# Copies of x and the first eight splits ahead of the main loop's, a last bank in two halves, and stationary parts moved by 32 bytes

## The chip, the cores and the metric

The kernel runs on one core of a Trainium2 chip. The metric is the device time of one execution in microseconds (us), the median of several runs.

## What is computed

One layer of a decoder trunk on x of 256 tokens by 2048, in float32:

```
h = rms_norm(x, g_mix);  q, k, v of 16 heads = h @ w_in
x = x + concat(diff_attention, moba_attention, dilated_attention) @ w_out
x = x + memory_cross_attention(rms_norm(x), rms_norm(mem), w_cq, w_ckv, w_co)
x = x + (silu(causal_dwconv3(h @ w_gate)) * (h @ w_up_half)) @ w_down,  h = rms_norm(x, g_ffn)
out = rms_norm(x, g_final)
```

The weights w_in, w_out, w_ckv, w_cq, w_co, w_up and w_down come to some 220 MB and are read once.

## The kernel before, in words

**Products in parts.** A float32 operand is split into a high part (a copy rounded to float32r, made on ScalarE) and a low part (the remainder, made on VectorE). A product of two operands is the sum of high by high, high by low and low by high, all accumulated in one PSUM bank. Activations lie in hT with the high part of a block of 128 rows in the first 256 columns and the low part in the next 256.

**Pieces, halves and steps.** All weights are streamed in pieces of 1 MB (2048 columns of 128 partitions), each into one of four buffers raw (NRAW = 4), by SyncE's queue. A piece has two halves of 1024 columns. split_hi (line 142) casts a half on ScalarE, split_lo (line 149) makes its low part on VectorE; there are five buffers of each (NSPLIT = 5), so that half i waits until the matmuls of an earlier half have been done. The main loop (lines 1023 to 1040) has one step for each half: it allots and issues loads (line 127), splits the half that is LEAD = 4 ahead, runs what is due before the step, runs the matmuls of the step and then what is due after it. The functions before(i, f) and after(i, f) put work at those places. The order in which instructions are written is the order on each engine's queue; nothing reorders it.

**The start.** x comes in as 16 blocks of 128 by 256; a block is multiplied by its gain and split into hT on ScalarE (line 194) and VectorE (line 197); put_x does it for two blocks. The loads of x and of pieces 0 to 2 are written alternately on SyncE's queue, the load of piece 3 follows. A fourth buffer of raw is taken by a tile named hold: POOL writes one column of it (line 951), and VectorE copies that column before step 8 (line 952), which ends the tile's life. So piece 3 goes into piece 0's buffer, and so on. Blocks 0 to 3 and halves 0 and 1 are split ahead of the loop. Then lines 981 and 982 put two blocks of x and one half after each of the steps 0 to 5:

```
    for i in range(6):
        after(i, lambda i=i: (put_x(2 * i + 4), split(i + 2)))
```

The loop itself splits half 8 at step 4, half 9 at step 5 and so on, ahead of the step's matmuls; what is due after a step is written behind them.

The first group of 512 columns takes steps 0 to 7. In steps 0 to 2 the eight high matmuls of 512 columns (line 295) come first and then the eight low ones of 256 (line 302); from step 3 on they alternate in pairs. A group has four PSUM banks of a pool of five (NACC = 5). At the end of step 7 each bank is emptied by a copy on ScalarE (line 354) and an add on VectorE (line 355). Step 8 begins the next group of columns with four banks, the first of which is the fifth of the pool. Squares of x are summed beside steps 5 to 9 (line 223 on ScalarE, line 227 on VectorE).

**The down projection and the tail.** For it the activations are the stationary operand (ah, al, 128 by 128) and the weights the moving one, 512 columns at a time (lines 851 to 853). All eight banks hold outputs: two tiles of 128 tokens by four quarters of 512 columns. The last TAIL = 2 rows of blocks are kept back, and for each bank in turn their matmuls are run at the end, so that banks become ready one after the other. Each is added to x on VectorE (line 890) and squared and summed on ScalarE (line 265); after the last of a tile the sums give a factor (lines 899 to 901 on VectorE, a power on POOL at line 903), and finish multiplies each quarter by it and stores it. gains multiplies some quarters by g_final ahead of that (line 898).

**Places in memory.** A tile's place is rounded up to 32 bytes. The high and low weight parts hi and lo begin at a multiple of 64 bytes; hT, and in the down projection ah and al, begin 32 bytes past one. The tile gfin lies ahead of ah and al.

Of the kernel before, what the change touches and what calls it, by code (L numbers as in the profile page):

```python
# [11 lines left out]
F32 = mybir.dt.float32  # L12
# [50 lines left out]
def trunk(ctx, tc, x, mem, w_in, w_out, diff_lambda, rel_bias_table, w_cq, w_ckv, w_co, w_up, conv, w_down,  # L63
# [30 lines left out]
    def small(n, name, bufs=4):  # L94
        return tmp.tile([P, n], F32, tag=f"sm_{name}", name=name, bufs=bufs)
# [62 lines left out]
    def before(i, f):  # L158
        pre.setdefault(i, []).append(f)

    def after(i, f):
        post.setdefault(i, []).append(f)
# [100 lines left out]
    def square_sum(src, acc, n=512):  # L263
        junk = tmp.tile([P, 512], mybir.dt.bfloat16, tag="junk", name="junk", bufs=1)
        ACT.activation(junk[:, :n], src, AF.Square, accum_out=acc)
# [557 lines left out]
    def xtok(t, c):  # L823

        return xT[:, 4 * c + 2 * t:4 * c + 2 * t + 2, :].rearrange("p k n -> p (k n)")
# [17 lines left out]
        hi, lo = parts[k]  # L843
        DVE.tensor_tensor(lo, ffn["a"][:, k, :], hi.bitcast(F32), op=ALU.subtract)

    def down_mm(p, k, h, t, n):
        hi, lo = p.parts[h]
        ah, al = (a[:, t * P:(t + 1) * P] for a in parts[k])
        o = outs[t, 2 * h + n]
        wh, wl = hi[:, n * 512:(n + 1) * 512], lo[:, n * 512:(n + 1) * 512]  # L850
        PE.matmul(o, ah, wh, start=(k == 0), stop=False)  # L851
        PE.matmul(o, ah, wl, start=False, stop=False)  # L852
        PE.matmul(o, al, wh, start=False, stop=(k == KF - 1))  # L853

    ss3 = small(8, "ss3", 1)
    fin = {}

    def finish(n, t, og, r):
        col = slice(n * 512, (n + 1) * 512)
        if t and n % 2:  # L860
            DVE.scalar_tensor_tensor(og[:, col], xtok(t, n), r, gfin["t"][:, col], op0=ALU.mult, op1=ALU.mult)
        elif t or n < 2:
            ACT.activation(og[:, col], og[:, col], AF.Copy, scale=r)
        else:
            (DVE, POOL)[n - 2].tensor_scalar_mul(og[:, col], og[:, col], r)
        SP.dma_start(out[t * P:(t + 1) * P, col], og[:, col])

    def down(k):
        def f(p, h):
            if k == 0 and h == 0:  # L870
                for t in range(NT):
                    for n in range(4):
                        outs[t, n] = any_tile()
            fin[k] = p
            if k < KF - TAIL:
                for t in range(NT):
                    for n in range(2):
                        down_mm(p, k, h, t, n)
            elif k == KF - 1 and h == 1:
                done = None  # L880
                for t in range(NT):
                    og = wpool.tile([P, 2 * HALF], F32, tag="raw", name="raw", bufs=NRAW)
                    ms = small(2, "msf")
                    ss = ss3[:, 4 * t:4 * t + 4]
                    for n in range(4):
                        for kk in range(KF - TAIL, KF):
                            down_mm(fin[kk], kk, n // 2, t, n % 2)
                        col = slice(n * 512, (n + 1) * 512)
                        xc = xtok(t, n)
                        DVE.tensor_tensor(xc, outs[t, n], xc, op=ALU.add)  # L890
                        square_sum(xc, ss[:, n:n + 1])
                        if done:
                            for m in ((3, 0, 1), (2,), (), ())[n]:
                                finish(m, *done)
                        gains = ((), (0,), (), (2,)) if t else ((0,), (1,), (2,), (3,))
                        for m in gains[n]:
                            col = slice(m * 512, (m + 1) * 512)
                            DVE.tensor_tensor(og[:, col], xtok(t, m), gfin["t"][:, col], op=ALU.mult)
                    DVE.reduce_sum(ms[:, 0:1], ss[:, :3], axis=AX.X)
                    DVE.tensor_scalar(ms[:, 0:1], ms[:, 0:1], 1.0 / D, EPS, op0=ALU.mult, op1=ALU.add)  # L900
                    DVE.scalar_tensor_tensor(ms[:, 1:2], ss[:, 3:4], 1.0 / D, ms[:, 0:1], op0=ALU.mult, op1=ALU.add)
                    r = small(1, "rfin")
                    POOL.tensor_tensor(r, ms[:, 1:2], mhalf, op=ALU.pow)
                    done = t, og, r
                for n in range(4):
                    finish(n, *done)
        return f

# [4 lines left out]
    gfin = {}  # L913

    def load_final():
        gfin["t"] = ffn["p"].tile([P, D], F32, name="gfin")
        SP.dma_start(gfin["t"], bass.AP(tensor=g_final.tensor, offset=g_final.offset, ap=[[0, P], [1, D]]))

    after(startF + 10, load_final)
# [26 lines left out]
    load_x(12, 4)  # L946

    hold = wpool.tile([P, 2 * HALF], F32, tag="raw", name="raw", bufs=NRAW)  # L950
    POOL.memset(hold[:, :1], 0.0)
    before(8, lambda: DVE.tensor_copy(small(1, "held", 1), hold[:, :1]))


    warm = acc_tile()
    for _ in range(24):
        PE.transpose(warm[:, :P], ident, ident)
# [20 lines left out]
    split(1)  # L978
    load(pieces[3])
    nload = 4  # L980
    for i in range(6):
        after(i, lambda i=i: (put_x(2 * i + 4), split(i + 2)))
    for c in range(4):
        square_part(c + 5, "x", c, lambda c=c: xpart(c))
    norm_factors(10, "x")
# [87 lines left out]
```

## Time and profile before

| | us |
|---|---|
| median of 3 runs (1252.23 to 1252.81) | 1252.4 |
| the profiled execution | 1252.27 |
| its span, first to last instruction | 1250.5 |
| TensorE busy in the span | 1235.8 |
| VectorE busy | 830.8 |
| ScalarE busy | 630.0 |

The profile tells for one execution when each instruction began and how long it took. In its views PE is TensorE (matmuls), PEld its weight loads, DVE VectorE, ACT ScalarE, POOL GpSimd and SP SyncE. L149 is line 149 of the kernel, lo<-raw,hi says that the tile lo is written from raw and hi, and a bracket tells how long the engine was idle before and what ended that. Matmuls are pipelined: a matmul's duration is longer than the distance to the next one's start, and it is the distance that counts in a stream. Times in the views are from the start of the span.

### The profile page before, as it was taken

What the parts mean: (1) busy time and instruction counts of PE and PEld (TensorE: products, weight loads), DVE (VectorE), ACT (ScalarE), POOL (GpSimd) and SP (SyncE); (2) the same over time, 40 slices, a digit from 0 to 9 for tenths busy, and PEclk for the clock granted to TensorE, in tenths of its full rate; (3) what the DMA queues carried; (4) which work ended last, traced back from release to release, by engine and by line L of the source; (5) the groups of instructions that cost most, each with busy time, mean ns of one, the idle gap of its engine ahead of it and who ended that gap; (6) DMA issues with size and microseconds to landing.
All of it is one profiled execution on the core that took longest, in us unless ns stands there. A gap on an engine that the chain in (4) does not pass through costs nothing.

```text
span 1250.5 us, 17611 instructions
## 1 busy us (share of the span) xinstructions
PE 1235.8 (99%) x6928; PEld 1072.4 (86%) x6928; DVE 830.8 (66%) x1351; ACT 630.0 (50%) x979; POOL 12.3 (1%) x23
## 2 busy tenths in 40 slices
PE   8999999999999999999999999999999999999997
PEld 7888888988888899888888888888888888888885
DVE  5755676576568877876767768667776854445445
ACT  6544555556455656545445444444444544444444
POOL 0000000000000000000000000000000000000000
PEclk9999999999999999999999999999999999999998
DMA  7855554555566555565556565565556555555541
GB/s 275 273 172 191 189 170 159 182 184 156 177 227 217 170 169 164 204 206 169 170 201 196 175 202 190 183 201 184 187 180 202 192 193 180 200 176 194 187 150 68
DMA packets 104835, 233.26 MB, mean 187 GB/s; under 512 B 4208, under 2 KB 14768, under 8 KB 98992
## 3 DMA queue, kind: packets, MB, share of 16 engines
q1 hardware_dynamic: 104576, 231.85, 55.3%
q8 instruction: 54, 0.88, 0.3%
q10 hardware_dynamic: 144, 0.26, 0.1%
q14 instruction: 29, 0.24, 0.1%
q0 software_dynamic: 32, 0.02, 0.0%
HBM read 230.00 MB, written 2.12 MB: 186 GB/s over the span
## 4 chain that ended last, share of the span: by engine, by line
issue 58%; PE 37%; DMA 2%; DVE 2%; ACT 0%; POOL 0%; DVEq 0%; POOLq 0%; SPq 0%; ACTq 0%
PE acc L295 16%; PE acc L302 8%; PE acc L341 3%; PE acc L343 3%; PE acc L342 3%; DMA raw<-in_w_in 1%; PE at L401 1%; DMA xin<-in_x 1%; DVE lo L149 1%; PE at L420 0%; PE at L444 0%; DVE hT L197 0%; PE acc L298 0%; PE acc L297 0%; PE at L472 0%
## 5 line engine op out<-in xcount | busy, mean ns | idle before, releaser
L149 DVE TENSOR_TENSOR lo<-raw,hi 128x1024 fp32r<-128x1024 f32 x423 | 517.1, 1223 | 360.0 <-ACT hi L142 359.5
L142 ACT CAST hi<-raw 128x1024 fp32r<-128x1024 f32 x423 | 442.8, 1048 | 473.1 <-PE acc L295 272.4
L295 PE MATMUL acc<-hT,hi 128*128 128x512 f32 x1776 | 625.4, 395 | 3.5 <-ACT hi L142 3.3
L302 PE MATMUL acc<-hT,lo 128*128 128x256 f32 x1840 | 512.0, 280 | 0.6 <-DVE lo L149 0.6
L295 PEld LDWEIGHTS acc<-hT,hi 128*128 128x128 f32 x1776 | 334.4, 188 | 78.1 <-ACT hi L142 3.7
L302 PEld LDWEIGHTS acc<-hT,lo 128*128 128x128 f32 x1840 | 345.3, 188 | 1.4 <-DVE lo L149 1.2
L295 PE MATMUL at<-hT,hi 128*128 128x512 f32 x528 | 187.5, 392 | 0.0
L302 PE MATMUL at<-hT,lo 128*128 128x256 f32 x528 | 147.6, 280 | 0.0
L295 PEld LDWEIGHTS at<-hT,hi 128*128 128x128 f32 x528 | 99.1, 188 | 21.8
L302 PEld LDWEIGHTS at<-hT,lo 128*128 128x128 f32 x528 | 99.2, 188 | 0.0
L851 PE MATMUL acc<-hi,ah 128*128 128x512 f32 x220 | 87.8, 399 | 0.0
L853 PE MATMUL acc<-hi,al 128*128 128x512 f32 x220 | 86.7, 394 | 0.0
L852 PE MATMUL acc<-lo,ah 128*128 128x512 f32 x220 | 86.2, 392 | 0.0
L341 PE MATMUL acc<-hi,hT 128*128 128x256 f32 (+1 forms) x224 | 75.0, 335 | 0.0
L343 PE MATMUL acc<-hi,hT 128*128 128x256 f32 (+1 forms) x224 | 73.9, 330 | 0.0
L342 PE MATMUL acc<-lo,hT 128*128 128x256 f32 (+1 forms) x224 | 73.8, 330 | 0.0
L851 PE MATMUL at<-hi,ah 128*128 128x512 f32 x132 | 52.7, 399 | 0.0
L853 PE MATMUL at<-hi,al 128*128 128x512 f32 x132 | 52.0, 394 | 0.0
L788 ACT ACTIVATE y<-y 128x256 f32<-128x256 f32 x44 | 18.4, 419 | 66.3 <-DVE y L784 66.3
L852 PE MATMUL at<-lo,ah 128*128 128x512 f32 x132 | 51.7, 392 | 0.0
L853 PEld LDWEIGHTS acc<-hi,al 128*128 128x128 f32 x220 | 41.3, 188 | 10.8
L852 PEld LDWEIGHTS acc<-lo,ah 128*128 128x128 f32 x220 | 41.3, 188 | 9.8
(159 smaller groups left out, 1003.2 us busy)
## 6 DMA issues: line engine op xcount, KB each, us to landing
raw<-in_w_up SPq DMA_DIRECT2D x88, 1024.0 KB, 5.0
raw<-in_w_in SPq DMA_DIRECT2D x45, 1024.0 KB, 5.2
raw<-in_w_down SPq DMA_DIRECT2D x44, 1024.0 KB, 4.9
raw<-in_w_out SPq DMA_DIRECT2D x12, 1024.0 KB, 5.3
raw<-in_w_ckv SPq DMA_DIRECT2D x8, 1024.0 KB, 5.6
raw<-in_w_out SPq DMA_DIRECT2D x8, 512.0 KB, 4.9
raw<-in_w_cq SPq DMA_DIRECT2D x4, 1024.0 KB, 5.3
raw<-in_w_co SPq DMA_DIRECT2D x4, 1024.0 KB, 5.2
```

The lines of the kernel that those rows point to most:

```text
L142: ACT.copy(hi, p.raw[:, h * HALF:(h + 1) * HALF])
L149: DVE.tensor_tensor(lo, p.raw[:, h * HALF:(h + 1) * HALF], hi.bitcast(F32), op=ALU.subtract)
L295: PE.matmul(accs[n], w, x, start=(i == 0), stop=False)
L302: PE.matmul(accs[n][:, :S], lo[:, j, n * P:(n + 1) * P], src()[:, korder[i], :S], start=False, stop=(i == len(korder) - 1))
L341: PE.matmul(o, xh, hi[:, j, :], start=(i == 0), stop=False)
L342: PE.matmul(o, xh, lo[:, j, :], start=False, stop=False)
L343: PE.matmul(o, xl, hi[:, j, :], start=False, stop=(i == len(korder) - 1))
L401: PE.matmul(out, a[u], b[w], start=first and i == 0, stop=last and i == 2)
L788: after(cur[0] + 1 + n, lambda: ACT.activation(gate[k], gate[k], AF.Silu))
L851: PE.matmul(o, ah, wh, start=(k == 0), stop=False)
L852: PE.matmul(o, ah, wl, start=False, stop=False)
L853: PE.matmul(o, al, wh, start=False, stop=(k == KF - 1))
```

## The change

The two blocks of x and one half that stood after each of the steps 0 to 5 stand, two such groups each, after the steps 0 to 2. The tile hold and its copy are gone. In the tail, the last quarter of the second tile is computed in two halves of 256 columns; the second half's share of the kept back rows goes to a PSUM tile of its own and is added after the whole bank. The order and the engines of the last multiplications and stores differ: for the first tile POOL takes two quarters (VectorE had one of them), for the second tile ScalarE takes quarters 0 and 1 and VectorE 2 and 3, stored in the order 2, 0, 3, 1. gfin has 8 more columns that nobody reads, which moves ah and al by 32 bytes. The tile ss3 of sums grows from 8 to 10 columns.

```diff
--- before.py
+++ after.py
@@ -843,27 +843,34 @@
         hi, lo = parts[k]
         DVE.tensor_tensor(lo, ffn["a"][:, k, :], hi.bitcast(F32), op=ALU.subtract)
 
-    def down_mm(p, k, h, t, n):
+    def down_mm(p, k, h, t, n, c0=0, c1=512, own=None):
         hi, lo = p.parts[h]
         ah, al = (a[:, t * P:(t + 1) * P] for a in parts[k])
-        o = outs[t, 2 * h + n]
-        wh, wl = hi[:, n * 512:(n + 1) * 512], lo[:, n * 512:(n + 1) * 512]
-        PE.matmul(o, ah, wh, start=(k == 0), stop=False)
+        o, first = (outs[t, 2 * h + n][:, c0:c1], 0) if own is None else (own, KF - TAIL)
+        wh, wl = (a[:, n * 512 + c0:n * 512 + c1] for a in (hi, lo))
+        PE.matmul(o, ah, wh, start=(k == first), stop=False)
         PE.matmul(o, ah, wl, start=False, stop=False)
         PE.matmul(o, al, wh, start=False, stop=(k == KF - 1))
 
-    ss3 = small(8, "ss3", 1)
+    ss3 = small(10, "ss3", 1)
     fin = {}
 
     def finish(n, t, og, r):
         col = slice(n * 512, (n + 1) * 512)
-        if t and n % 2:
-            DVE.scalar_tensor_tensor(og[:, col], xtok(t, n), r, gfin["t"][:, col], op0=ALU.mult, op1=ALU.mult)
-        elif t or n < 2:
+        if t:
+            if n < 2:
+                ACT.activation(og[:, col], og[:, col], AF.Copy, scale=r)
+            else:
+                DVE.scalar_tensor_tensor(og[:, col], xtok(t, n), r, gfin["t"][:, col], op0=ALU.mult, op1=ALU.mult)
+        elif n < 2:
             ACT.activation(og[:, col], og[:, col], AF.Copy, scale=r)
         else:
-            (DVE, POOL)[n - 2].tensor_scalar_mul(og[:, col], og[:, col], r)
+            POOL.tensor_scalar_mul(og[:, col], og[:, col], r)
         SP.dma_start(out[t * P:(t + 1) * P, col], og[:, col])
+
+    def gained(og, t, n):
+        col = slice(n * 512, (n + 1) * 512)
+        DVE.tensor_tensor(og[:, col], xtok(t, n), gfin["t"][:, col], op=ALU.mult)
 
     def down(k):
         def f(p, h):
@@ -881,28 +888,33 @@
                 for t in range(NT):
                     og = wpool.tile([P, 2 * HALF], F32, tag="raw", name="raw", bufs=NRAW)
                     ms = small(2, "msf")
-                    ss = ss3[:, 4 * t:4 * t + 4]
-                    for n in range(4):
+                    ss = ss3[:, 5 * t:5 * t + 5]
+
+                    parts_of = ((0, 0, 512), (1, 0, 512), (2, 0, 512)) + (((3, 0, 256), (3, 256, 512)) if t else ((3, 0, 512),))
+                    for i, (n, c0, c1) in enumerate(parts_of):
+                        own = any_tile()[:, :c1 - c0] if c0 else None
                         for kk in range(KF - TAIL, KF):
-                            down_mm(fin[kk], kk, n // 2, t, n % 2)
-                        col = slice(n * 512, (n + 1) * 512)
-                        xc = xtok(t, n)
-                        DVE.tensor_tensor(xc, outs[t, n], xc, op=ALU.add)
-                        square_sum(xc, ss[:, n:n + 1])
+                            down_mm(fin[kk], kk, n // 2, t, n % 2, c0, c1, own)
+                        xc = xtok(t, n)[:, c0:c1]
+                        if own is None:
+                            DVE.tensor_tensor(xtok(t, n), outs[t, n], xtok(t, n), op=ALU.add)
+                        else:
+                            DVE.tensor_tensor(xc, own, xc, op=ALU.add)
+                        square_sum(xc, ss[:, i:i + 1], c1 - c0)
                         if done:
-                            for m in ((3, 0, 1), (2,), (), ())[n]:
+                            for m in ((2, 0), (3, 1), (), (), ())[i]:
                                 finish(m, *done)
-                        gains = ((), (0,), (), (2,)) if t else ((0,), (1,), (2,), (3,))
-                        for m in gains[n]:
-                            col = slice(m * 512, (m + 1) * 512)
-                            DVE.tensor_tensor(og[:, col], xtok(t, m), gfin["t"][:, col], op=ALU.mult)
+                        if not t or n < 2:
+                            gained(og, t, n)
                     DVE.reduce_sum(ms[:, 0:1], ss[:, :3], axis=AX.X)
                     DVE.tensor_scalar(ms[:, 0:1], ms[:, 0:1], 1.0 / D, EPS, op0=ALU.mult, op1=ALU.add)
-                    DVE.scalar_tensor_tensor(ms[:, 1:2], ss[:, 3:4], 1.0 / D, ms[:, 0:1], op0=ALU.mult, op1=ALU.add)
+                    if t:
+                        DVE.scalar_tensor_tensor(ms[:, 0:1], ss[:, 3:4], 1.0 / D, ms[:, 0:1], op0=ALU.mult, op1=ALU.add)
+                    DVE.scalar_tensor_tensor(ms[:, 1:2], ss[:, i:i + 1], 1.0 / D, ms[:, 0:1], op0=ALU.mult, op1=ALU.add)
                     r = small(1, "rfin")
                     POOL.tensor_tensor(r, ms[:, 1:2], mhalf, op=ALU.pow)
                     done = t, og, r
-                for n in range(4):
+                for n in (2, 0, 3, 1):
                     finish(n, *done)
         return f
 
@@ -913,7 +925,7 @@
     gfin = {}
 
     def load_final():
-        gfin["t"] = ffn["p"].tile([P, D], F32, name="gfin")
+        gfin["t"] = ffn["p"].tile([P, D + 8], F32, name="gfin")[:, :D]
         SP.dma_start(gfin["t"], bass.AP(tensor=g_final.tensor, offset=g_final.offset, ap=[[0, P], [1, D]]))
 
     after(startF + 10, load_final)
@@ -946,12 +958,6 @@
     load_x(12, 4)
 
 
-
-    hold = wpool.tile([P, 2 * HALF], F32, tag="raw", name="raw", bufs=NRAW)
-    POOL.memset(hold[:, :1], 0.0)
-    before(8, lambda: DVE.tensor_copy(small(1, "held", 1), hold[:, :1]))
-
-
     warm = acc_tile()
     for _ in range(24):
         PE.transpose(warm[:, :P], ident, ident)
@@ -978,8 +984,10 @@
     split(1)
     load(pieces[3])
     nload = 4
-    for i in range(6):
-        after(i, lambda i=i: (put_x(2 * i + 4), split(i + 2)))
+
+    for i in range(3):
+        for j in range(2):
+            after(i, lambda h=2 * i + j: (put_x(2 * h + 4), split(h + 2)))
     for c in range(4):
         square_part(c + 5, "x", c, lambda c=c: xpart(c))
     norm_factors(10, "x")
```

## Rows read from the trace of the kernel before

**Rows 1.** The page's busy times by engine, share of the span.

```profile
PE 1235.8 (99%) x6928; PEld 1072.4 (86%) x6928; DVE 830.8 (66%) x1351; ACT 630.0 (50%) x979; POOL 12.3 (1%) x23
```

**Rows 2.** Windows: length, busy PE, PEld, DVE, ACT, POOL, granted clock, DMA share, GB/s.

```profile
23.30:25.50 2.20, 0.06 (x1) 0.00 (x0) 0.57 (x1) 1.65 (x3) 0.00 (x0) 1.00 0.46 169
25.60:32.30 6.70, 4.96 (x14) 3.88 (x15) 6.59 (x9) 6.58 (x9) 0.00 (x0) 0.50 0.29 77
```

**Rows 3.** Timeline of TensorE, 22.5 to 36.3: start us, duration us, instruction, [idle before].

```profile
23.08 0.28 PE L302 MATMUL acc<-hT,lo 128*128 128x256 f32 x1
26.70 0.79 PE L295 MATMUL acc<-hT,hi 128*128 128x512 f32 x1 [3.34 <-ACT hi L142]
28.14 0.58 PE L302 MATMUL acc<-hT,lo 128*128 128x256 f32 x1 [0.65 <-DVE lo L149]
...
32.71 0.40 PE L295 MATMUL acc<-hT,hi 128*128 128x512 f32 x1
...
36.18 0.39 PE L295 MATMUL acc<-hT,hi 128*128 128x512 f32 x1
```

**Rows 4.** Timeline of ScalarE, 16 to 29.

```profile
23.85 1.05 ACT L142 CAST hi<-raw 128x1024 fp32r<-128x1024 f32 x1 [6.29 <-DMA raw<-in_w_in]
24.80 0.90 ACT L194 ACTIVATE hT<-xin 128x256 fp32r<-128x256 f32 x2
25.61 1.98 ACT L142 CAST hi<-raw 128x1024 fp32r<-128x1024 f32 x2
```

**Rows 5.** The tile raw, 8 to 20.5: SyncE's loads, and their time to landing.

```profile
L127 SPq DMA_DIRECT2D raw<-in_w_in x3: 367/368/368, 10.4 to 19.0; - x3
...
DMA to landing us min/median/max: 7.4/9.3/10.7
```

**Rows 6.** Timeline of VectorE, 24 to 44.

```profile
26.07 0.87 DVE L197 SCALAR_TENSOR_TENSOR hT<-xin,hT 128x256 fp32r<-128x256 f32 x2
...
35.02 1.50 DVE L355 TENSOR_TENSOR mg<-acc,mg 128x256 f32<-128x256 f32 x4
...
40.55 1.22 DVE L149 TENSOR_TENSOR lo<-raw,hi 128x1024 fp32r<-128x1024 f32 x1
41.68 1.14 DVE L236 TENSOR_TENSOR sq<-sq 128x512 f32<-128x512 f32 x2
```

**Rows 7.** Timeline of TensorE, four stretches: distances between the starts of matmuls.

```profile
9.73 1.57 PE L295 MATMUL acc<-hT,hi 128*128 128x512 f32 x6
11.13 0.28 PE L302 MATMUL acc<-hT,lo 128*128 128x256 f32 x1
...
104.20 0.29 PE L342 MATMUL acc<-lo,hT 128*128 128x256 f32 x1
104.33 0.28 PE L343 MATMUL acc<-hi,hT 128*128 128x256 f32 x1
...
104.92 0.29 PE L342 MATMUL acc<-lo,hT 128*128 128x256 f32 x1
...
482.22 0.28 PE L298 MATMUL acc<-hT,hi 128*128 128x256 f32 x1
...
483.27 0.28 PE L298 MATMUL acc<-hT,hi 128*128 128x256 f32 x1
...
1195.05 0.40 PE L851 MATMUL at<-hi,ah 128*128 128x512 f32 x1
...
1195.75 0.40 PE L851 MATMUL acc<-hi,ah 128*128 128x512 f32 x1
```

**Rows 8.** Timelines of VectorE, ScalarE and POOL in the tail, 1229 to 1251.

```profile
1241.45 0.69 DVE L890 TENSOR_TENSOR xin<-acc,xin 128x512 f32<-128x512 f32 x1 [0.52 <-PE acc L853]
...
1243.10 0.16 DVE L901 SCALAR_TENSOR_TENSOR msf<-ss,msf 128x1 f32<-128x1 f32 x1
...
1242.23 0.63 ACT L265 ACTIVATE junk<-xin 128x512 bf16<-128x512 f32 x1 [0.43 <-DVE xin L890]
...
1238.52 1.68 POOL L865 TENSOR_SCALAR raw<-raw,rfin 128x512 f32<-128x512 f32 x1
```

## The prediction, on record before the change was run

> **What bounds the kernel now.** I read the page's busy times first: TensorE is busy for 1235.8 of a span of 1250.5 us [rows 1], so nothing between the first weights and the last bank can gain much unless a matmul itself gets shorter. Only 14.7 us are idle, and they lie at the two ends. The windows say more: between 25.6 and 32.3 us the granted clock is 0.50, the lower level of 1.2 GHz, against 1.00 before [rows 2]. TensorE's timeline shows why: step 5 ends with the matmul at 23.08, the next starts at 26.70 after an idle 3.34 us, its low part waits until 28.14, and step 7 begins only at 32.71 [rows 3]. From 32.71 to 36.18 there are ten pairs of a 512- and a 256-wide matmul, 0.347 us each; a step is eight, 2.78 us. Step 6 should begin at 23.20 (23.08 and a 256-wide one's 0.12) and so end at 25.98; it ended 6.7 us later, of which some 2 us are the low clock's and the rest idle.
>
> What held it is seen on ScalarE's queue. After the high part of half 5 it stands for 6.29 us until a weight load has landed, and only then come two blocks of x and further casts [rows 4]. By the code's order the cast at 23.85 is half 8, the first of piece 4, issued by the main loop at step 4; half 6, which step 6 needs, is queued behind it at 25.61. The load rows give three issues from 10.4 to 19.0 and 10.7, 9.3, 7.4 us to landing [rows 5], in order of issue: piece 3 is there at 21.1, piece 4 at 23.8 (the cast waits for it), piece 5 at 26.4. So step 6's data lay there from 21.1 on, behind a cast that wanted later data.
>
> **The change, part by part. (a) The start.** With the six groups after steps 0 to 2, ScalarE's order is 5, 6, 7, 8, 9, and the blocks of x go with them. Half 6 then starts at 21.1 and ends at 22.2. VectorE's low part ends at 23.4; the first low matmul of step 6 would be at 23.43, so at most 0.1 us of wait is left. Half 7 follows the pair of x blocks (0.81 us by the starts 24.80 and 25.61), half 8 starts at 23.85, half 10 at 26.7: pieces 4 and 5 have just landed.
>
> Then something else is late. Step 8 opens the second group of columns. Its first bank is free; its second, 0.69 us (two pairs) later, is one that VectorE must first empty (line 355). Now that matmul is at 36.18 and the adds run from 35.02, 0.375 us each [rows 3, 6], so the slack is 0.8 us. Afterwards VectorE has from 22.2 on: the lows of halves 6 to 11, one add of squares, two x blocks, and only then those adds. Large ones follow each other in 1.14 us (40.55 to 41.68), the x pair takes 0.8 us [rows 6]: 7 x 1.14 + 0.8 = 8.8 us, and 0.2 us of waits for half 10: 31.2, first add done at 31.6. TensorE wants that bank at 23.2 + 0.1 + 2 x 2.78 + 0.69 = 29.55. A new wait of 2.1 us. Start: -6.7 + 0.1 + 2.1 = **-4.5 us**. Between: if piece 3 lands a us sooner, its buffer being free, VectorE starts sooner and the wait is 1.1, -5.5; with no wait at step 8, -6.6.
>
> Taking the held buffer away removes POOL's memset and VectorE's copy of one column, which no other engine waits for but SyncE's fourth load after them, and moves SyncE's loads up by one buffer: piece 3 needs no release, pieces 4 to 6 take the buffers of 0 to 2 and go out from 10.4 to 19.0, when 3 to 5 go now [rows 5]. The loads behind them, and step 6's five small ones, are issued sooner too. The queue serves in order by the landings above, so I count nothing; if it shares, see the fourth rival.
>
> **(b) The tail.** The last bank becomes two halves. Twelve matmuls of 256 columns at 0.120 us (line 342's, six in 0.72) instead of six at 0.233 [rows 7]: the end comes 0.04 us later. After it stand now an add of 512 columns (0.69), a square of 0.63 with its read-out, the factor at 1243.10, POOL's power, two multiplications and four stores [rows 8]. The last add has 256 columns (0.375, as line 355): -0.3. The last square is 0.2 shorter, but waits 0.15 for the first half's on ScalarE. The additional small sum lies under that square; the gains of the last two quarters are no longer made ahead, but VectorE now multiplies both there as it did two. Sum **-0.3 us**. POOL takes a second multiplication of 1.68 us for the first tile, 1240.2 to 1241.9 (1238.52 and two times 1.68); the power needs POOL 0.3 us before 1243.1. If VectorE's traffic makes it 0.9 longer, that cover is gone and each further 0.1 costs 0.1.
>
> **(c) The 32 bytes.** ah and al now begin 32 bytes past a multiple of 64, and will begin on one. hT stays where it is (the sums grow by 32 bytes, the dropped column gives 32 back). No row shows both operands on 64, so I bound it by rows 7. Down projection now: three matmuls of 512 columns in 0.70 us, 233.3 ns each. A stationary part on 64 with a moving one off it: 256 columns, nine in 1.05 us, 116.7 ns, against 120.0 ns the other way round (line 342): 3.3 ns less, times 1056 matmuls = -3.5 us. Pairs of 512 and 256, also with the stationary part on 64 [rows 3]: two thirds of 0.347 us are 231.3 ns, 2.0 less, -2.1 us. Six of 512 in a row at the start, the same way round: 1.40 us, 233.3 ns, 0. A loss isn't excluded either. I take **-2.1 us**, the pairs' value: the same width in a steady stretch, and between the other two.
>
> The Trainium skill speaks against this part: "SBUF — State Buffer", Specifications (TRN2), gives lines of 16 bytes with a penalty for each crossing. 32 bytes are two whole lines, so by it nothing changes and the sum is 1247.6. The row of six 512-wide ones agrees (233.3 ns on either side), the 256-wide ones (3.3 ns apart) don't.
>
> **Sum.** -4.5 - 0.3 - 2.1 = -6.9 us against the profiled execution's 1252.27 (its span of 1250.5 and 1.8 around it): 1245.4. The median of the runs is 0.13 above it: **1245.5**. A difference of 0.2% (2.5 us) is about what a measurement of this kernel can tell from none.
>
> **Rivals.**
> - *The 32 bytes do nothing.* For it: the row of 512-wide ones, the nearest in width. Against it: the 256-wide ones. Time: 1245.5 + 2.1 = 1247.6. Chance 0.27. By the Trainium skill's page above, this is what happens.
> - *No or a shorter wait at step 8, or a full alignment gain.* If piece 3 lands a us sooner or VectorE's order proves looser, the start gives 5.5 to 6.6; if every matmul gains 3.3 ns, (c) gives 3.5. Each ends at 1243.5 to 1244.5, both at 1242. Against it: the loads were the limit until 24 us. Chance 0.15.
> - *The new wait lowers the clock.* Now 3.34 idle us lie before the low stretch [rows 2, 3]; 2.1 might be enough. From 28.14 to 32.71 the low clock took 4.57 us for 2.55 us of work, so +2.0: 1247.5, without (c) 1249.6. Chance 0.10.
> - *The start gives nothing.* With three loads out early, if the queue shares rather than serves in order, piece 3 lands as late as piece 5 does now (26.4) and step 6 starts at 28.8, as now. Only (b) and (c) are left: 1250.0. The landings in order speak against it. Chance 0.05.
> - *Slower: both operands on 64 meet.* The place is the down projection's read of its two operands: if each matmul has to let the other's read pass, I price it by the 256-wide ones of line 342, single ones of which take 0.13 us against the mean of 0.12 [rows 7]: 10 ns, 1056 x 10 = +10.6 us, and -4.8 from (a) and (b): 1258.2. From 7 ns a matmul on (7.4 us) it is slower by over 0.2%. No row has this pairing. Chance 0.05.
>
> **How the numbers follow.** The forecast (-4.5, -0.3, about -2) has 0.38. Faster by over 0.2% are it, the first two rivals and most of the clock's: 0.89. Within 0.2%: the fourth and the clock's rest, 0.06. Slower: 0.05. The range reaches from 1242.0 (both gains full) to 1249.5 (low clock without (c)) and leaves out the last two rivals and the ends.
>
> **What would show it.** Right for (a): ScalarE casts without a long gap after half 5, the idle time at 23 gone, TensorE idle some 2 us near 29.5 for line 355. Wrong, if step 6 still waits over 1 us or no wait stands at step 8. Right for (b): two squares after the last bank, the last factor 0.3 us nearer to the last matmul. Right for (c): three down-projection matmuls in 0.69 us instead of 0.70, and the projection 2 us shorter; wrong, if it is 0.70 still. The forecast falls as a whole if the start gives under 2.5 us, or the triple takes 0.71 or more.

## The result, and the profile after

The kernel after takes 1243.05 us (median of six runs, 1242.94 to 1244.53) where the kernel before took 1252.32 beside it: a ratio of 0.9929, 95% interval 0.9919 to 0.9939, so 9.3 us or 0.7% faster. The forecast was 1245.5 with a range of 1242.0 to 1249.5. The profiled execution is the longest of the six, 1244.53 with a span of 1242.7; why it is 1.5 us longer than the median is seen below. Two of the runs further down, of the start alone and of the tail alone, had one execution far longer than the others (1344.84 and 2482.97 us), and their medians are taken without it.

TensorE is busy for 6 us less than in [rows 1], with six matmuls more (the last bank's halves):

```profile
PE 1229.7 (99%) x6934; PEld 1072.0 (86%) x6934; DVE 830.9 (67%) x1351; ACT 630.3 (51%) x981; POOL 14.2 (1%) x23
```

**The start.** ScalarE's timeline, the answer to [rows 4] (start, duration, instruction, idle time before it and what ended it):

```profile
20.83 1.05 ACT L142 CAST hi<-raw 128x1024 fp32r<-128x1024 f32 x1 [2.69 <-DMA raw<-in_w_in]
21.79 0.90 ACT L194 ACTIVATE hT<-xin 128x256 fp32r<-128x256 f32 x2
22.60 2.95 ACT L142 CAST hi<-raw 128x1024 fp32r<-128x1024 f32 x3
```

The first cast is now half 6. It waits for piece 3 only, 2.69 us in place of 6.29, and three further casts follow the x blocks at once. VectorE's timeline, the answer to [rows 6], is closed from then on:

```profile
21.92 1.23 DVE L149 TENSOR_TENSOR lo<-raw,hi 128x1024 fp32r<-128x1024 f32 x1 [2.36 <-ACT hi L142]
23.06 0.88 DVE L197 SCALAR_TENSOR_TENSOR hT<-xin,hT 128x256 fp32r<-128x256 f32 x2
23.85 4.85 DVE L149 TENSOR_TENSOR lo<-raw,hi 128x1024 fp32r<-128x1024 f32 x4
28.62 1.22 DVE L227 TENSOR_TENSOR sq<-sq 128x1024 f32<-128x1024 f32 x1
29.75 1.22 DVE L149 TENSOR_TENSOR lo<-raw,hi 128x1024 fp32r<-128x1024 f32 x1
30.89 1.41 DVE L355 TENSOR_TENSOR mg<-acc,mg 128x256 f32<-128x256 f32 x4
```

And TensorE's, the answer to [rows 3]:

```profile
23.08 0.39 PE L295 MATMUL acc<-hT,hi 128*128 128x512 f32 x1
...
29.20 0.28 PE L302 MATMUL acc<-hT,lo 128*128 128x256 f32 x1
31.36 0.71 PE L295 MATMUL acc<-hT,hi 128*128 128x512 f32 x1 [1.88 <-DVE mg L355]
...
32.08 0.63 PE L295 MATMUL acc<-hT,hi 128*128 128x512 f32 x1
...
32.72 0.63 PE L295 MATMUL acc<-hT,hi 128*128 128x512 f32 x1
...
35.11 0.39 PE L295 MATMUL acc<-hT,hi 128*128 128x512 f32 x1
...
35.46 0.39 PE L295 MATMUL acc<-hT,hi 128*128 128x512 f32 x1
```

The idle 3.34 us at step 6 are gone: the pairs run on to 29.20. Then the new wait stands where it was expected, at the second bank of step 8, for the adds of line 355. Behind it the pairs take 0.64 us (32.08 to 32.72) until about 34.6 and 0.35 after 35.11. The windows name the cause, the granted clock (rows as in [rows 2]); 0.50 is its lower level, 1.2 GHz:

```profile
29.00:32.00 3.00, 1.12 (x6) 0.71 (x5) 3.00 (x6) 3.00 (x7) 0.00 (x0) 0.91 0.85 202
32.00:35.00 3.00, 3.00 (x12) 2.57 (x11) 3.00 (x4) 1.37 (x2) 0.00 (x0) 0.52 1.02 366
```

**The 32 bytes.** Two down-projection matmuls of line 851 in TensorE's timeline, ten triples apart:

```profile
1195.02 0.39 PE L851 MATMUL acc<-hi,ah 128*128 128x512 f32 x1
...
1201.89 0.39 PE L851 MATMUL at<-hi,ah 128*128 128x512 f32 x1
```

A triple takes 6.87 / 10 = 0.687 us, against 0.70 in [rows 7].

**The tail.** Timelines of TensorE, VectorE, ScalarE and POOL, the answer to [rows 8]:

```profile
1233.40 0.28 PE L853 MATMUL acc<-hi,al 128*128 128x256 f32 x1
...
1233.30 0.68 DVE L900 TENSOR_TENSOR xin<-acc,xin 128x512 f32<-128x512 f32 x1
1234.08 0.42 DVE L902 TENSOR_TENSOR xin<-acc,xin 128x256 f32<-128x256 f32 x1
...
1235.31 0.16 DVE L913 SCALAR_TENSOR_TENSOR msf<-ss,msf 128x1 f32<-128x1 f32 x1 [0.28 <-ACT junk L265]
...
1234.23 0.42 ACT L265 ACTIVATE junk<-xin 128x256 bf16<-128x256 f32 x1
...
1234.77 0.42 ACT L265 ACTIVATE junk<-xin 128x256 bf16<-128x256 f32 x1
...
1230.85 3.59 POOL L868 TENSOR_SCALAR raw<-raw,rfin 128x512 f32<-128x512 f32 x2
```

The last matmul ends at 1233.68, the last factor begins 1.63 us later. Before, it was 1.69 (matmul's end 1241.41, factor 1243.10). Of the gain of 0.3 only 0.06 is there.

### The profile page after: what moved, and what is told of

Read it like the earlier page. It is cut to its first block, busy times and chain, and to the rows that moved or that the text cites. A ratio compares the mean times of both kernels' runs of the same rounds, so it can differ in the third digit from the quotient of the medians.

```text
span 1242.7 us, 17626 instructions
## 1 busy us (share of the span) xinstructions
PE 1229.7 (99%) x6934; PEld 1072.0 (86%) x6934; DVE 830.9 (67%) x1351; ACT 630.3 (51%) x981; POOL 14.2 (1%) x23
## 4 chain that ended last, share of the span: by engine, by line
issue 58%; PE 37%; DVE 2%; DMA 1%; ACT 0%; POOL 0%; SPq 0%; POOLq 0%; DVEq 0%; ACTq 0%
PE acc L295 16%; PE acc L302 8%; PE acc L341 3%; PE acc L343 3%; PE acc L342 3%; DMA raw<-in_w_in 1%; PE at L401 1%; DVE lo L149 1%; PE at L420 0%; DMA xin<-in_x 0%; PE at L444 0%; PE acc L298 0%; PE acc L297 0%; DVE hT L197 0%; PE at L472 0%
## 5 line engine op out<-in xcount | busy, mean ns | idle before, releaser
L851 PE MATMUL acc<-hi,ah 128*128 128x512 f32 (+1 forms) x222 | 87.0, 392 | 0.0
L853 PE MATMUL acc<-hi,al 128*128 128x512 f32 (+1 forms) x222 | 86.6, 390 | 0.0
L852 PE MATMUL acc<-lo,ah 128*128 128x512 f32 (+1 forms) x222 | 85.7, 386 | 0.0
```

What stands on the lines that cost most here:

```text
L851: PE.matmul(o, ah, wh, start=(k == first), stop=False)
```

## The experiments

All were timed beside the kernel before, whose medians were 1252.0 to 1252.5.

### Each part alone, and the kernel after once more

The start alone, on the kernel before (ss3 grows to 10 columns here too, which makes up for the column that is dropped, so that nothing else moves):

```diff
-    hold = wpool.tile([P, 2 * HALF], F32, tag="raw", name="raw", bufs=NRAW)
-    POOL.memset(hold[:, :1], 0.0)
-    before(8, lambda: DVE.tensor_copy(small(1, "held", 1), hold[:, :1]))
-    for i in range(6):
-        after(i, lambda i=i: (put_x(2 * i + 4), split(i + 2)))
+    for i in range(3):
+        for j in range(2):
+            after(i, lambda h=2 * i + j: (put_x(2 * h + 4), split(h + 2)))
```

> The kernel before with the part on the start alone (the groups two each after steps 0 to 2, the held buffer gone; the tail and the places of all tiles as before). If the prediction's term for the start is right without a fall of the clock: 4.5 us less than before, 1247.9 by a median of 1252.4, an idle time of about 2 us for the add of line 355 at step 8, and the matmuls behind it at their former distance. If the new wait at step 8 lowers the clock in every execution, as it did in the profile of the kernel after (the matmuls behind it at half the distance's rate until 34.9): about 3.1 us less, 1249.3. If the whole of the stall is won: 6.6 us less, 1245.8.

The tail alone, on the kernel before: the change's down_mm, finish, gained and the loop over parts_of, with the held buffer kept and all places as before.

```diff
-                    for n in range(4):
+                    for i, (n, c0, c1) in enumerate(parts_of):
...
-    before(8, lambda: DVE.tensor_copy(small(1, "held", 1), hold[:, :1]))
+    before(8, lambda: DVE.tensor_copy(lam, hold[:, :1]))
```

> The kernel before with the part on the tail alone (the last bank in two halves and the other division of the last multiplications; start and places as before). By the prediction 0.3 us less, 1252.1. By the profile of the kernel after, in which the last factor began 1.63 us after the last matmul's end (1.69 before) and 9.0 us (9.1 before) lay from there to the end of the span: 0.1 us less at most, not to be told from no change. If VectorE, with a small sum more, delays the factor, up to 0.3 us more.

The 32 bytes alone, on the kernel before:

```diff
-        gfin["t"] = ffn["p"].tile([P, D], F32, name="gfin")
+        gfin["t"] = ffn["p"].tile([P, D + 8], F32, name="gfin")[:, :D]
```

> The kernel before with the 32 bytes alone (gfin 8 columns wider, so that the down projection's stationary parts begin on a multiple of 64 bytes). If the place is what shortened the triple of down-projection matmuls from 700 to 686.7 ns in the kernel after: 13.3 ns times 352 triples = 4.7 us less, 1247.7. By the prediction's term 2.1 us less, 1250.3. If the place does nothing and the triples became shorter by another part of the change (other addresses of the last bank, the loads' other timing): no change, 1252.4, and triples of 700 ns. The Trainium skill, "SBUF — State Buffer", Specifications (TRN2), has lines of 16 bytes, by which 32 bytes more change nothing.

The kernel after once more, with no edit but an empty line:

> The kernel after, unchanged but for an empty line, profiled again. If the clock falls behind the wait at step 8 in some executions alone: a profile with the wait of about 1.9 us for line 355 at 29.5 and the matmuls behind it at their distance of 0.347 us a pair, and a profiled time near 1243.0. If it falls in each: pairs of 0.64 us until about 34.9 again, and the difference of 1.5 us between the profiled execution (1244.5) and the others (1243.0) has another cause.

Measured, against 1252.5 beside them: the start alone 1247.75 (ratio 0.9962, 95% interval 0.9949 to 0.9976), so -4.8 us; the tail alone 1252.08 (0.9995, 0.9986 to 1.0004), -0.4 us, no change that can be told; the 32 bytes alone 1247.16 (0.9955, 0.9942 to 0.9969), -5.3 us; the kernel after again 1243.13 (0.9924, 0.9912 to 0.9937). The parts add up to -10.5 against -9.4 for the whole, within their intervals.

In the kernel with the 32 bytes alone the triple takes 687 ns (two matmuls ten triples apart):

```profile
1190.73 0.39 PE L851 MATMUL at<-hi,ah 128*128 128x512 f32 x1
...
1197.60 0.39 PE L851 MATMUL acc<-hi,ah 128*128 128x512 f32 x1
```

So the triples are 13.3 ns x 352 = 4.7 of its 5.3 us. Its low-clock stretch is also shorter: the granted clock from 25 to 32 us is 0.76 on average, and 0.54 in the kernel before. Why, nothing in it shows.

The kernel with the start alone, TensorE's timeline and then a window:

```profile
31.37 0.50 PE L295 MATMUL acc<-hT,hi 128*128 128x512 f32 x1 [1.83 <-DVE mg L355]
```

```profile
32.00:35.00 3.00, 3.00 (x19) 2.63 (x19) 3.00 (x4) 1.84 (x3) 0.00 (x0) 1.00 1.04 381
```

And the kernel after, profiled again:

```profile
31.33 0.50 PE L295 MATMUL acc<-hT,hi 128*128 128x512 f32 x1 [1.22 <-DVE mg L355]
```

```profile
32.00:35.00 3.00, 3.00 (x19) 2.66 (x18) 3.00 (x4) 1.85 (x3) 0.00 (x0) 1.00 1.05 382
```

The wait is there, the clock stays at 1.00 and 19 matmuls fit where 12 did. So the fall of the clock is a matter of the single execution: it makes the first profile's 1244.5 out of 1243.0. In all profiles with this wait (the others are below) the matmul behind it begins at 31.33 to 31.63 (32.52 with hT moved, where piece 3 landed late and half 6 was cast at 21.98 only), whether TensorE stood for 1.07 us or 1.88. The adds of line 355 set that moment; TensorE's earlier timing only says how long it waits. An earlier piece 3 doesn't bring the adds nearer. In this profile half 6 was cast 1.1 us sooner than in the first one, but VectorE then stood for ScalarE's later casts (0.64 us before half 8, 0.49 before half 10), and the adds began at 30.85, where they had begun at 30.89. ScalarE's timeline, then VectorE's:

```profile
19.71 1.05 ACT L142 CAST hi<-raw 128x1024 fp32r<-128x1024 f32 x1 [1.80 <-DMA raw<-in_w_in]
```

```profile
27.44 1.23 DVE L149 TENSOR_TENSOR lo<-raw,hi 128x1024 fp32r<-128x1024 f32 x1 [0.49 <-ACT hi L142]
...
30.85 1.41 DVE L355 TENSOR_TENSOR mg<-acc,mg 128x256 f32<-128x256 f32 x4
```

### Is the wait at step 8 the last one?

Three of the first group's banks are taken from the other pool of PSUM tiles, so that step 8 finds four free ones (edit of the kernel after):

```diff
+    first_banks = [at_tile, at_tile, at_tile, acc_tile]
+    def first_bank():
+        return first_banks.pop(0)()
...
-            wstat_chunk(w_in, col0 + c * 512, lambda: hT["h"], lambda n, a, c=c: puts[4 * c + n](n, a))
+            wstat_chunk(w_in, col0 + c * 512, lambda: hT["h"], lambda n, a, c=c: puts[4 * c + n](n, a),
+                        bank=first_bank if col0 == 0 and c == 0 else acc_tile)
```

> The kernel after, with the first group's first three banks taken from the other pool of PSUM tiles, so that step 8 finds four free banks and needs no evacuation. If what holds TensorE at 29.5 is the bank alone (theory): the wait of 1.2 to 1.9 us for line 355 is gone, the clock has nothing to fall behind, and the kernel takes 1.2 to 1.9 us less than the kernel after, 1241.2 to 1241.9 by 1243.1. If TensorE is held there or a step later by the casts or loads in any case (rival): the wait appears before a low part of step 8 or 9 instead, and the time stays at 1243.1.

Measured: 1242.54 (0.9923, 0.9910 to 0.9935), 0.6 us less than the kernel after, which lies inside the spread of the runs and not in the 1.2 to 1.9 expected. The wait for line 355 is gone, and another has come, seven us later. TensorE's timeline:

```profile
38.35 0.58 PE L241 MATMUL at<-ones,sq 128*128 128x1 f32 x4 [1.01 <-ACT hi L142]
```

The view names ScalarE's cast, which had long been done. Line 241 reads the folded squares, and VectorE's timeline has these until 38.20:

```profile
37.06 1.14 DVE L236 TENSOR_TENSOR sq<-sq 128x512 f32<-128x512 f32 x2
38.13 1.22 DVE L149 TENSOR_TENSOR lo<-raw,hi 128x1024 fp32r<-128x1024 f32 x1
```

So those sums were put one step later, on top of that edit:

```diff
-        after(i, total)
-        before(i + 1, column)
+        late = 1 if key == "x" else 0
+        after(i + late, total)
+        before(i + 1 + late, column)
```

> The kernel after with the free banks for step 8 and the sums of squares over the partitions (line 241) a step later, after step 11. With the banks alone a wait of 1.0 us stands before line 241, which needs VectorE's folded squares at 38.1. If that is the last wait of the start: 1.0 us less than with the banks alone, 1241.5 by 1242.5, no idle time of TensorE of over 0.1 us between 8 and 60 us. If VectorE's backlog meets TensorE again behind it (the low part of half 11 or 12): the wait moves once more and the time stays at 1242.5.

Measured: 1241.45 (0.9916, 0.9903 to 0.9930), the fastest of all. Its windows:

```profile
29.00:32.00 3.00, 3.00 (x20) 2.63 (x19) 3.00 (x5) 3.00 (x7) 0.00 (x0) 1.00 0.96 213
32.00:35.00 3.00, 3.00 (x20) 2.63 (x19) 3.00 (x5) 1.85 (x3) 0.00 (x0) 1.00 1.02 364
35.00:40.00 5.00, 5.00 (x32) 4.42 (x30) 4.97 (x6) 2.68 (x3) 0.00 (x0) 1.00 0.86 289
```

TensorE is busy without a gap, and it has no idle time of over 0.1 us from 8 to 60 us. By the medians the change's start left 1.7 us (1243.1 to 1241.45), in two waits behind one engine's queue. The ratios' intervals still overlap (0.9912 to 0.9937 for the kernel after); that both waits are gone is read from the traces.

### Order or buffer?

The kernel before, with the start's order alone and the held buffer kept:

```diff
-    for i in range(6):
-        after(i, lambda i=i: (put_x(2 * i + 4), split(i + 2)))
+    for i in range(3):
+        for j in range(2):
+            after(i, lambda h=2 * i + j: (put_x(2 * h + 4), split(h + 2)))
```

> The kernel before with the order of the start alone (two groups after each of the steps 0 to 2), the held buffer kept. If the order is what won the start (theory): half 6 is cast when piece 3 has landed (21.0 in the kernel before), step 6 begins without a wait, and the time is that of the whole start, 1247.8, or up to 1 us more, because piece 6 now waits for the held buffer (issued near 30, landed near 34.6) and half 12's cast and the last squares stand behind it, which the sum over the tokens (line 241, after step 10) may have to wait for. If the buffer is what won it (rival): step 6 still waits some 3 us and the time is 1250 or more.

Measured: 1248.13 (0.9970, 0.9959 to 0.9982), 0.4 us above the start as a whole and not to be told from it. ScalarE's timeline, and TensorE's:

```profile
20.31 1.05 ACT L142 CAST hi<-raw 128x1024 fp32r<-128x1024 f32 x1 [1.79 <-DMA raw<-in_w_in]
```

```profile
31.48 0.50 PE L295 MATMUL acc<-hT,hi 128*128 128x512 f32 x1 [1.68 <-DVE mg L355]
```

Half 6 is cast as early, and the wait at step 8 is the same. The order won the start. Of the expectation's details one missed: piece 6 was not late, it landed at 29.9, and what waited for the held buffer was piece 9, issued at 32.5 behind the copy at 32.3, which nobody needed yet.

### What in the tail ate the gain?

Quarter 1 of the second tile is not multiplied by g_final ahead (edit of the kernel after):

```diff
-            if n < 2:
+            if n < 1:
                 ACT.activation(og[:, col], og[:, col], AF.Copy, scale=r)
...
-                        if not t or n < 2:
+                        if not t or n < 1:
                             gained(og, t, n)
```

> The kernel after with quarter 1 of the second tile not multiplied by g_final ahead (ScalarE's later multiplication of it goes to VectorE, three of 0.70 us there and one on ScalarE). If VectorE's queue is what cost the gain in the tail (the add of the second half begins 0.40 us after the last matmul's end, with VectorE busy without a gap before it): the adds of the last two parts begin 0.3 us earlier, the last factor 1.3 us after the last matmul's end in place of 1.63, and the fourth store is issued 0.2 to 0.3 us earlier. If the delay has another cause (a matmul's result is readable only so late): still 0.40 and 1.63 us, and the third multiplication on VectorE ends about when the fourth store went out before. In time 0 to 0.3 us less than 1243.1, which the runs can't tell; the trace does.

Measured: 1243.13, as the kernel after. Timelines of TensorE, VectorE and ScalarE:

```profile
1232.06 0.28 PE L853 MATMUL acc<-hi,al 128*128 128x256 f32 x1
...
1232.46 0.42 DVE L902 TENSOR_TENSOR xin<-acc,xin 128x256 f32<-128x256 f32 x1
...
1233.88 0.16 DVE L913 SCALAR_TENSOR_TENSOR msf<-ss,msf 128x1 f32<-128x1 f32 x1 [0.38 <-ACT junk L265]
...
1231.44 0.71 ACT L866 ACTIVATE raw<-raw,rfin 128x512 f32<-128x512 f32 x1
1232.06 0.61 ACT L265 ACTIVATE junk<-xin 128x512 bf16<-128x512 f32 x1
...
1233.34 0.42 ACT L265 ACTIVATE junk<-xin 128x256 bf16<-128x256 f32 x1
```

The last add begins 0.12 us after the matmul's end (1232.34) in place of 0.40: VectorE's queue was indeed late. But the factor comes only 0.09 us nearer, 1.54 us after the matmul. Now ScalarE is last: its square of the first half and the read-out behind it must be done before the second one can start, 1232.80 to 1233.34, and the factor waits 0.38 us for that. ScalarE is late since it multiplies a quarter of the first tile at 1231.44 (line 866): the third square, whose add had ended at 1231.65, begins at 1232.06. In the kernel before ScalarE made both such multiplications ahead of the second square; the change puts one of them between the second and the third. Two queues in a row were full; freeing one shows the other. Moving that multiplication was not tried.

### What is it about the place?

The kernel after with 16 additional columns in place of 8, so that ah and al move 64 bytes from where they were:

```diff
-        gfin["t"] = ffn["p"].tile([P, D + 8], F32, name="gfin")[:, :D]
+        gfin["t"] = ffn["p"].tile([P, D + 16], F32, name="gfin")[:, :D]
```

> The kernel after with gfin 16 columns wider in place of 8: ah and al lie 64 bytes on from where they lay before, 32 bytes past a multiple of 64 again. If the multiple of 64 decides: triples of 700 ns as in the kernel before and the 13.3 ns x 352 = 4.7 us lost again, 1247.8 by 1243.1. If any move away from the old place helps (another distance to the weight parts): triples of 687 ns and 1243.1.

The kernel after with hT, and all that is allotted behind ss3 up to gfin, moved by 32 bytes and ah, al kept:

```diff
-    ss3 = small(10, "ss3", 1)
+    ss3 = small(18, "ss3", 1)
...
-        gfin["t"] = ffn["p"].tile([P, D + 8], F32, name="gfin")[:, :D]
+        gfin["t"] = ffn["p"].tile([P, D], F32, name="gfin")
```

> The kernel after with everything that is allotted behind ss3 moved by 32 bytes and gfin without its additional columns: ah and al stay on a multiple of 64, and hT, the moving operand of the some 2300 pairs of a 512- and a 256-wide matmul, now begins on one too (the stationary weight parts did already). If the place of either operand costs (theory A): pairs of 343 to 345 ns in place of 347, 5 to 9 us less than the kernel after, 1234 to 1238. If only the stationary operand's place costs (theory B): pairs of 347 ns and no change, 1243.1. If both on 64 were bad in the pairs: longer; the down projection, where both lie on 64, speaks against it.

The kernel after with the moving weight parts 32 bytes on, in the down projection alone:

```diff
-        hi = wpool.tile([P, HALF], F32R, tag="hi", name="hi", bufs=NSPLIT)
-        lo = wpool.tile([P, HALF], F32R, tag="lo", name="lo", bufs=NSPLIT)
+        at = 0 if p.extra is None else 8
+        hi, lo = (wpool.tile([P, HALF + 16], F32R, tag=t, name=t, bufs=NSPLIT)[:, at:at + HALF] for t in ("hi", "lo"))
```

> The kernel after with the weight parts, the moving operand, moved by 32 bytes in the down projection alone (buffers 16 columns wider, the parts 8 columns in); ah and al stay on a multiple of 64, and the pairs and the other products keep their places. So far the triple took 700 ns with the stationary part off 64 and the moving one on it, 687 with both on it; the pair takes 347 ns with the stationary part on 64 and the moving one off it, 353.6 with both on it. If the stationary part's place alone decides for the triple: 687 ns and 1243.1. If a moving operand off 64 helps a stationary one on 64, as in the pairs (6.6 ns a pair): triples of 674 to 680 ns, 2.4 to 4.7 us less, 1238.4 to 1240.7. If the triple wants both on 64: 694 to 700 ns, 1245.5 to 1247.8.

The same wider buffers with nothing moved in them:

```diff
-        at = 0 if p.extra is None else 8
+        at = 0
```

> The kernel after with the weight buffers 16 columns wider, the parts in them not moved: the starts of the buffers lie 4160 bytes apart in place of 4096 (still multiples of 64), what is allotted behind them 640 bytes on. It parts the two things that the run with the weight parts moved by 32 bytes changed at once (there: triples of 699 ns, and pairs of 350 in place of 347 though their operands' remainders by 64 were as before). If the remainder by 64 decides for the triple and the wider buffers cost the pairs: triples of 687 ns, pairs of 350, 2300 times 2.8 ns = 6.4 us more than the kernel after, 1249.5. If the wider buffers cost the triple too (its 699 ns then not the 32 bytes'): triples of 690 to 700 ns, 1250.5 to 1254. If the pairs were longer there for another reason: pairs of 347 ns and 1243.1.

Measured: 64 bytes 1247.68 (0.9965, 0.9953 to 0.9978); hT moved 1254.43 (1.0020, 1.0011 to 1.0029), slower than the kernel before; weights moved 1253.28 (1.0011, 1.0002 to 1.0020); wider buffers alone 1252.63 (1.0003, 0.9994 to 1.0013). TensorE's timeline with 64 bytes, two matmuls ten triples apart:

```profile
1195.28 0.40 PE L851 MATMUL acc<-hi,ah 128*128 128x512 f32 x1
...
1202.27 0.40 PE L851 MATMUL acc<-hi,ah 128*128 128x512 f32 x1
```

0.699 us: the gain is lost, 4.6 us, as the multiple of 64 would have it. With hT moved, two matmuls ten pairs apart:

```profile
699.90 0.40 PE L295 MATMUL acc<-hT,hi 128*128 128x512 f32 x1
...
703.43 0.40 PE L295 MATMUL acc<-hT,hi 128*128 128x512 f32 x1
```

0.353 us a pair, with both operands on a multiple of 64. That is 6.1 ns more (averaged over the trace) times 2300, 14.0 us, and the products in which hT is the stationary operand (lines 341 to 343) give back 2.7: +11.3, as measured. With the wider buffers alone, ten pairs and ten triples:

```profile
699.87 0.39 PE L295 MATMUL acc<-hT,hi 128*128 128x512 f32 x1
...
703.36 0.39 PE L295 MATMUL acc<-hT,hi 128*128 128x512 f32 x1
...
1194.78 0.39 PE L851 MATMUL acc<-hi,ah 128*128 128x512 f32 x1
...
1201.72 0.40 PE L851 MATMUL acc<-hi,ah 128*128 128x512 f32 x1
```

0.349 and 0.694 us (0.697 over the whole projection), though every operand has the same remainder by 64 as in the kernel after. So the multiple of 64 doesn't decide either, and the run with the weights moved says nothing of the 32 bytes: its 699 ns are 2 more than with the wider buffers alone. What differs are the places within a larger span and the distances between the operands. From the program's allocation and the distances over each whole trace:

| | weights' start mod 256 | other operand's start mod 256 | spacing, ns |
|---|---|---|---|
| triple before | 192 | ah 96 | 700 |
| triple after | 192 | ah 128 | 687 |
| triple, 64 bytes | 192 | ah 160 | 700 |
| triple, wider buffers | 0, 64, 128, 192 by turns | ah 0 | 697 |
| pair before, after | 192 | hT 96 | 347 |
| pair, hT moved | 192 | hT 128 | 353 |
| pair, wider buffers | 0, 64, 128, 192 by turns | hT 224 | 350 |

The weights' column is that of the high parts, hi. In the last row the buffers differ among themselves: the 512-wide matmul takes 231.2, 232.2, 236.2 and 229.1 ns with its weights at 192, 0, 64 and 128. Only the last equals the kernel after's 229.3, and there the weights lie at 192. The same place of the second operand, 128, is the best for the triple and the worse one for the pair. By which rule, these runs don't settle.

## Why the prediction was right, and where it wasn't

**The whole:** 1243.05 lies in the range, 2.5 us under the forecast. That difference is mainly (c), which gave 2.6 us more than its term. The time lies 0.5 us under the band of the second rival, "no or a shorter wait at step 8, or a full alignment gain" (1243.5 to 1244.5), and of that rival it is the alignment half.

**(a) The start, -4.5: right**, and the steps with it. Alone it gave -4.8. The stall at step 6 is gone, the queue served the loads in order (the fourth rival falls), VectorE was late next, the adds of line 355 were done when the sum of its queue said (first add 31.6 predicted, next matmul at 31.36), and TensorE stood 1.88 us for them against 2.1. The branch "if piece 3 lands a us sooner" (-5.5) didn't hold: with half 6 cast 1.1 us sooner the adds began at 30.85 in place of 30.89. The experiments add that the order did it, not the freed buffer, and that this wait hid a second one of 1.0 us on the same queue.

**The clock (third rival):** in the first profile it came true, at the place and by the mechanism named; a low stretch from 31.5 to 34.9 cost 1.5 us, where 2.0 was put. In eight other profiles with a wait of 1.07 to 1.83 us there it didn't; 1.88 beside 1.83 makes no bound. The Trainium skill, "TensorE: Matmul & The Clock Gate", Part 1, says of a kernel's start that the number of slow matmuls varies from run to run. The two profiles of the kernel after show the like in mid-kernel (12 matmuls from 32 to 35 us in one, 19 in the other).

**(b) The tail, -0.3: failed**, in the step "the last add has 256 columns (0.375): -0.3". The add is shorter (0.42), but began 0.40 us after the last matmul, since VectorE was still at the whole bank's add, 0.68 us from 1233.30; before, it had stood idle for 0.52 us ahead of its last add [rows 8]. Splitting the bank put an add of full width in front of the short one, with a gain ahead of the add before it, and the sum treated VectorE as free. It treated ScalarE as nearly free, too: the wait for it was put at 0.15 us, and the second square began 0.27 us after its add's end. With VectorE freed, only 0.09 us came back, since ScalarE was full as well. POOL's cover held: two multiplications took 3.59 us, to 1234.44, with the power at 1235.55.

**(c) The 32 bytes, -2.1: the sign right, the size not.** The triple lost 13.3 ns, 4.4 ns a matmul, where 2.0 was taken and 3.3 was the bound: -4.7 us, outside it. What failed is the inference from other groups of matmuls. The pairs' 231.3 ns were taken for what a stationary operand on 64 gives, and that value itself was misread: two thirds of a pair is not its wide matmul, which takes 229.3 ns in the trace before (the narrow one 117.9). By 229.3 the term would have been -4.2 us. That would have been near by luck, as is the sign: pairs and triples answer to the place in opposite ways, and by the same inference hT on 64 was expected to gain or to change nothing, where it cost 11.3 us. The first rival, nothing from 32 bytes, falls with the run of that part alone. The Trainium skill's lines of 16 bytes ("SBUF — State Buffer", Specifications (TRN2)) gave no change; 687 against 700 ns disagrees, so those lines can't be all that counts in the place. The fifth rival, "both operands on 64 meet", was wrong for its place, the down projection. The pairs did take 6.1 ns more when both lay on 64, but that the two reads meet there isn't shown, and the wider buffers speak against 64 as the rule.

**The check** "the triple takes 0.69 instead of 0.70" came true; "the projection 2 us shorter" was 4.7.

## What to carry to other kernels

When a stall goes, add up the queue of the engine that comes next, up to the moment at which its result is wanted; here that sum placed the new wait within 0.3 us, and carried on to line 241 it might have found the second. A step made shorter at the end of a chain gains only if the engine is free when it starts: write the busy time ahead of it into the sum. In this kernel's streams of matmuls an operand's place was worth one or two per cent either way: try several places of each, one at a time, measure the distance between starts in every group that reads it, and distrust a rule inferred from another group.

## What was not expected of the hardware

A shift of 32 bytes of one operand changes the distance of 512-wide matmuls by 4.4 ns (triples, 233.3 to 228.9) or 5.6 ns (pairs' wide one, 229.3 to 234.9, longer with both operands on 64), and buffers 64 bytes further apart, with all behind them 640 bytes on, cost 9.5 us of 1243. The Trainium skill, "TensorE: Matmul & The Clock Gate", Back-to-back issue gap, gives an isolated distance of about 216 ns for 512 columns and about 131 in a sustained stream. Here the best triple's mean is 229 ns, longer than either.
